# The timeline simulator for the scheduler, and the last layer's Hyena and GLA gates projected early and parked in DRAM

## The chip, the cores and the metric

The kernel runs on one core of one Trainium2 chip. The metric is the device time of one execution in microseconds. The kernel before took 2607.05 us in the median of three runs (2606.05 to 2609.52). One further execution was profiled.

## The reference, cut to what matters

Two layers work on 256 latent and 256 context tokens of width 1024. Each layer is a half-step SwiGLU, then four token mixers side by side on one normalised input `u` (MLA, GLA, GQA and Hyena, in the code the branches a, b, c and d with the indices 0 to 3), then an output projection and a second half-step SwiGLU. What matters here is how the four mixers are merged:

```python
def merge(outs, gate_cols, w_branch):
    B, L, _ = gate_cols.shape
    g = jax.nn.sigmoid(gate_cols.reshape(B, L, N_BRANCH, D_MODEL))
    y = g[:, :, 0] * (outs[0] @ w_branch[0])
    for i in range(1, N_BRANCH):
        y = y + g[:, :, i] * (outs[i] @ w_branch[i])
    return y
```

`gate_cols` is a product of `u` with 4096 columns of the input projection. So a gate depends on `u` alone and not on its branch, while `outs[i] @ w_branch[i]` has to wait for the branch. In the last layer only the 256 latent tokens are merged.

## The kernel before, in words

All activations lie with channels on the partitions (eight tiles of 128 channels for the width of 1024). Every fp32 product is made of three matmuls of rounded halves (`mm3`, line 296): weight high by input high, high by low, low by high. So each weight has to be split on the chip. `weights` (L323) loads a raw tile of 128x1024 with a DMA of the SP queue (`raw`, L318, three buffers `wr`) and `pieces` (L328) splits it in two pieces of 512 columns: ScalarE casts the high part `wh` (L311), and a subtraction makes the low part `wl` (L312). There are eight buffers for each of the two. The subtraction runs on VectorE, or on GpSimd for every piece while `self.share` is 1, as it is in the last layer beside the Hyena and GLA chains and nowhere else.

`mixer` (L1339) orders a layer's mixers. In the last layer, `prep` projects what MLA, GLA and GQA need and runs beside the MLA and GQA chains. Then `weave` (L1326) runs two chains, `hyena` and `gla`, against a filler, `merges`: in each round it takes one step of each chain, issued with a priority 200 instructions earlier than its place (`first`), and one step of the filler. Hyena has 15 such steps and GLA 13. The filler has 16 steps: `merge` (L1294) of MLA (b = 0) and of GQA (b = 2), eight output tiles each. One step of `merge` in this layer (n = 256) is a gate projection of 24 matmuls with the two split pieces of its own weight, twelve matmuls of the branch product into the other half of the same PSUM bank, a tanh on ScalarE (L1314), and two operations of VectorE (L1316, L1319) that form (1 + tanh) times the product and add it to `y`. After the weave come, with nothing beside them, `merge` of Hyena (b = 3) and of GLA (b = 1), 16 steps again, and then the output projection `wo`.

The gates' PSUM tiles come from a pool of two banks (`acc0`); the tanh's result lies in a pool `m` of three buffers. Weight loads, spills to DRAM and reloads from DRAM all go through the SP queue.

The order of the instructions on each engine is not written by hand: the tile framework's scheduler lays them out when the program is built. It takes the instructions by priority (their place in the program, moved by `first` and `evac`) as a simulator says that their operands and buffers are ready. Each engine then runs its list strictly in that order.

Of the kernel before, what the change touches and what calls it, by code (L numbers as in the profile page):

```python
# [8 lines left out]
F32 = mybir.dt.float32  # L9
# [3 lines left out]
AF = mybir.ActivationFunctionType  # L13
ALU = mybir.AluOpType
# [3 lines left out]
P = 128  # L18
D = 1024
KD = 8  # L20
L = 256
# [198 lines left out]
class Net:  # L220
# [150 lines left out]
    def load(self):  # L371
        nc, A, c = self.nc, self.A, self.const

        def ld(name, shape, src, dt=F32):
            t = c.tile(shape, dt, name=name)
            nc.sync.dma_start(out=t, in_=src)
            return t

        cc = ld("cc", [P, KD, 2], A["cc"])
        vec = ld("vec", [P, NVEC], A["vec"])  # L380
        self.v = {n: vec[:, o:o + w] for n, (o, w) in VEC.items()}
        self.ident = ld("ident", [P, P], A["ident"])
        tab = ld("tab", [P, NTAB], A["tab"])
        self.tab = {n: tab[:, o:o + w] for n, (o, w) in TAB.items()}
        self.ones = c.tile([P, 1], F32, name="ones")
        nc.vector.memset(self.ones, 1.0)
        cs = c.tile([P, KD, 32], F32, name="cs")
        nc.vector.memset(cs, 0.0)
        th = c.tile([P, KD, 2], F32, name="th")
        nc.scalar.activation(th, cc, AF.Tanh, scale=0.5)  # L390
        nc.vector.tensor_scalar(out=th, in0=th, scalar1=1.0, scalar2=0.5, op0=ALU.add, op1=ALU.mult)
        nc.vector.tensor_mul(cs[:, :, 0:2], th, cc)
        self.cs = cs
        self.xd = [self.dram.tile([KD, P, NT], F32, name=f"xd{l}") for l in range(DEPTH)]
        self.sp = {}
        self.hs = self.dram.tile([DEPTH, 2, 4, P, 512], F32, name="hs")

    def load_x(self, src, n=NT):
# [892 lines left out]
        out.extend(dst)  # L1291


    def merge(self, l, b, ob, u, n, first=False, last=None):  # L1294
        nc, A = self.nc, self.A
        if first:
            self.y = self.packed("y", "y", n, KD)
        for mp in range(4):
            wb = self.weights(A["w_br"][l, b, mp], 1024)
            for e in range(2):  # L1300
                m = 2 * mp + e
                pg = self.psa(0, "gate")
                self.fm(pg, self.weights(A["w_gate"][l, b * KD + m], 1024), u, n)
                t = self.tl("m", "mt")
                if n == NT:
                    nc.scalar.activation(t[:, :n], pg[:, :n], AF.Tanh, scale=0.5)
                    p = self.psa(1, "br")
                else:
                    p = pg[:, n:]
                for k in range(4):  # L1310
                    self.mm3(p[:, :n], wb(e * 512 + k * P, P), (ob[k][0][:, :n], ob[k][1][:, :n]), k == 0, k == 3)
                with self.evac():
                    if n < NT:
                        nc.scalar.activation(t[:, :n], pg[:, :n], AF.Tanh, scale=0.5)  # L1314
                    y = self.y[m]
                    nc.vector.scalar_tensor_tensor(out=y if first else t[:, :n], in0=t[:, :n], scalar=1.0, in1=p[:, :n],  # L1316
                                                   op0=ALU.add, op1=ALU.mult)
                    if not first:
                        nc.vector.tensor_add(y, y, t[:, :n])  # L1319
                if last is not None:  # L1320
                    h, lo = self.pair("yh", "yh", n, "yl")
                    self.two(h[:, :n], lo[:, :n], y)
                    last.append((h, lo))
                yield

    def weave(self, chains, fill):  # L1326

        chains = list(chains)
        more = True
        while chains or more:  # L1330
            for c in list(chains):
                with self.first():
                    self.ahead = AHEAD
                    if next(c, 0) is not None:
                        chains.remove(c)
                    self.ahead = 0
            more = next(fill, 0) is None

    def mixer(self, l, u, last):  # L1339
        nseq = 1 if last else 2  # L1340
        self.phase("end" if last else "mix")
        nq, n = 2 * nseq, nseq * L
        oa, ob, oc, od, y = [], [], [], [], []
        if last:
            self.phase("end", "end1")
            prep = self.prep(l, u, nq)
            for _ in range(2 * HEAD):
                next(prep)
            self.weave([self.mla(l, nq, oa), self.gqa(l, nq, oc)], prep)
            self.phase("end", "end2")  # L1350
            self.share = SHARE_W

            def merges():
                yield from self.merge(l, 0, oa, u, n, first=True)
                yield from self.merge(l, 2, oc, u, n)

            self.weave([self.hyena(l, u, nseq, od), self.gla(l, nq, ob)], merges())
            self.share = 0
            for _ in self.merge(l, 3, od, u, n):
                pass  # L1360
        else:
            self.weave([self.hyena(l, u, nseq, od)], self.prep(l, u, nq))
            self.weave([self.mla(l, nq, oa)], self.merge(l, 3, od, u, n, first=True))
            self.weave([self.gqa(l, nq, oc)], self.merge(l, 0, oa, u, n))
            self.weave([self.gla(l, nq, ob)], self.merge(l, 2, oc, u, n))
        for _ in self.merge(l, 1, ob, u, n, last=y):
            pass
        self.load_x(self.xd[l], n)
        gt = self.gate(l, 1, 0.5)
        for m in range(KD):  # L1370
            w = self.weights(self.A["w_out"][l, m], 1024)
            p = self.psa(m % 2, "wo")
            self.fm(p, w, lambda k, c0, c1: (y[k][0][:, c0:c1], y[k][1][:, c0:c1]), n)
            self.resid(p, m, n, gt)
# [58 lines left out]
```

## Time and profile before

| what | value |
|---|---|
| median of three runs | 2607.05 us (2606.05 to 2609.52) |
| profiled execution, its own time | 2601.85 us |
| its span, first to last instruction | 2600.1 us |
| TensorE matmul busy | 2497.5 us (96%) |
| VectorE busy | 1696.6 us (65%) |
| ScalarE busy | 1091.1 us (42%) |
| GpSimd busy | 264.9 us (10%) |
| mean granted TensorE clock | 0.986 |

The profile is of one execution. PE stands for TensorE's matmuls, PEld for its weight loads, which overlap them, DVE for VectorE, ACT for ScalarE, POOL for GpSimd, SP for SyncE, which issues the DMAs. Times in rows are microseconds from the start of the span unless marked ns; `x` counts instructions. "a<-b" names the tile written and the tiles read. The program's names are kept: `gate` is the PSUM tile of a merge step, `dp` a Hyena projection, `AT`, `obT`, `pre`, `la` and `ab` belong to GLA, `Z`, `yi` and `yT` to Hyena.

### The profile page before, as it was taken

The page shows a single profiled execution, that of the slowest core. Times are in us where ns is not written, and L with a number is a line of the kernel's source. Part 1 is how long each engine was busy: PE and PEld are TensorE (multiplying, and loading weights), DVE is VectorE, ACT ScalarE, POOL GpSimd, SP SyncE. Part 2 cuts the span into 40 slices and gives each one's busy share as a digit, 9 for nine tenths or more (in the row PEclk, how much of TensorE's full clock was granted, in tenths as well). Part 3 has the DMA queues.
Part 4 walks back from the last instruction along what each step waited for, and adds up shares of the span by engine and source line. Part 5 has one row for each costly group of instructions (what it writes and reads, how often), then busy time and mean ns, then how long its engine had stood idle before and what let it go on. Part 6 is the DMA issues. An engine that isn't in the chain of part 4 may idle for free. (4 is left out here: it accounts for less than half of the span.)

```text
span 2600.1 us, 36866 instructions
## 1 busy us (share of the span) xinstructions
PE 2497.5 (96%) x13624; PEld 2058.8 (79%) x13624; DVE 1696.6 (65%) x3377; ACT 1091.1 (42%) x2127; POOL 264.9 (10%) x240
## 2 busy tenths in 40 slices
PE   6999999999999999999999999999999987899998
PEld 4778887887877667777888878888888777788998
DVE  5667858577547778746744466767458667776665
ACT  4333223333545554433232343232346664455554
POOL 2110003001000000020000030000020147401000
PEclk9999999999999999999999999999999999899999
DMA  7564535332313123245623244545353333356554
GB/s 253 176 213 170 190 128 192 134 108 100 126 57 122 61 88 106 89 156 174 205 97 97 86 158 146 178 146 174 102 187 130 114 120 122 114 161 210 177 184 124
DMA packets 122371, 369.01 MB, mean 142 GB/s; under 512 B 14090, under 2 KB 19660, under 8 KB 122192
## 3 DMA queue, kind: packets, MB, share of 16 engines
q1 hardware_dynamic: 122192, 366.66, 42.8%
q8 instruction: 107, 1.75, 0.3%
q14 instruction: 72, 0.59, 0.1%
HBM read 346.16 MB, written 20.45 MB: 141 GB/s over the span
## 5 line engine op out<-in xcount | busy, mean ns | idle before, releaser
L311 ACT CAST wh<-wr 128x512 fp32r<-128x512 f32 (+1 forms) x926 | 564.0, 613 | 1070.3 <-PE gu L301 396.0
L312 DVE TENSOR_TENSOR wl<-wr,wh 128x512 fp32r<-128x512 f32 (+1 forms) x854 | 577.1, 682 | 410.1 <-ACT wh L311 399.3
L301 PE MATMUL gu<-ul,wh 128*128 128x512 f32 (+1 forms) x1408 | 514.7, 366 | 2.5 <-DVE ul L542 2.5
L301 PE MATMUL gu<-uh,wh 128*128 128x512 f32 (+1 forms) x1408 | 512.3, 366 | 2.4 <-ACT uh L536 2.3
L301 PE MATMUL gu<-uh,wl 128*128 128x512 f32 (+1 forms) x1408 | 511.5, 364 | 1.3 <-DVE wl L312 1.3
L301 PE MATMUL dn<-hh,wh 128*128 128x512 f32 (+1 forms) x1408 | 389.5, 363 | 0.0
L301 PEld LDWEIGHTS gu<-ul,wh 128*128 128x128 f32 x1408 | 265.7, 189 | 58.4 <-DVE ul L542 9.3
L301 PEld LDWEIGHTS gu<-uh,wh 128*128 128x128 f32 x1408 | 265.8, 189 | 52.0 <-ACT uh L536 7.2
L301 PEld LDWEIGHTS gu<-uh,wl 128*128 128x128 f32 x1408 | 265.6, 189 | 44.0 <-DVE wl L312 1.7
L301 PEld LDWEIGHTS dn<-hh,wh 128*128 128x128 f32 x1408 | 252.6, 188 | 41.3
L301 PE MATMUL dn<-hh,wl 128*128 128x512 f32 (+1 forms) x704 | 255.3, 363 | 0.0
L502 POOL TENSOR_TENSOR nacc<-nacc,sq 128x512 f32<-128x512 f32 (+1 forms) x39 | 46.2, 1185 | 1745.1 <-ACT sq L500 1736.7
L301 PE MATMUL gate<-uh,wh 128*128 128x256 f32 (+1 forms) x768 | 202.3, 328 | 3.3 <-DVE y L1316 3.3
L464 DVE SCALAR_TENSOR_TENSOR aj<-aw,crow 128x1024 bf16<-128x1024 f32 x160 | 193.7, 1224 | 0.0
L301 PE MATMUL gate<-uh,wl 128*128 128x512 f32 (+1 forms) x512 | 177.0, 346 | 4.3 <-POOL wl L312 2.8
L301 PEld LDWEIGHTS dn<-hh,wl 128*128 128x128 f32 x704 | 132.3, 188 | 20.4
L301 PEld LDWEIGHTS gate<-uh,wh 128*128 128x128 f32 x768 | 132.0, 195 | 15.4 <-DVE y L1316 3.5
L301 PE MATMUL tm<-wh,uh 128*128 128x256 f32 x576 | 140.3, 288 | 1.6 <-ACT uh L536 1.0
L312 POOL TENSOR_TENSOR wl<-wr,wh 128x512 fp32r<-128x512 f32 x72 | 106.4, 1489 | 239.9 <-ACT wh L311 234.1
L301 PE MATMUL tm<-wl,uh 128*128 128x256 f32 x432 | 124.1, 287 | 0.0
L301 PEld LDWEIGHTS gate<-uh,wl 128*128 128x128 f32 x512 | 99.1, 194 | 15.9 <-POOL wl L312 3.0
L642 DVE SCALAR_TENSOR_TENSOR x<-dn,gt,x 128x256 f32<-128x256 f32 x168 | 74.4, 478 | 54.6 <-PE dn L301 54.6
(408 smaller groups left out, 3975.7 us busy)
## 6 DMA issues: line engine op xcount, KB each, us to landing
wr<-in_gu SPq DMA_DIRECT2D x176, 512.0 KB, 3.5
aw<-in_adat SPq DMA_DIRECT2D x80, 512.0 KB, 3.6
wr<-in_dn SPq DMA_DIRECT2D x64, 512.0 KB, 3.6
wr<-in_w_gate SPq DMA_DIRECT2D x64, 512.0 KB, 3.5
aw<-in_ada SPq DMA_DIRECT2D x48, 512.0 KB, 4.6
wr<-in_w_tm SPq DMA_DIRECT2D x36, 512.0 KB, 3.6
wr<-in_w_br SPq DMA_DIRECT2D x32, 512.0 KB, 3.5
wr<-in_dn SPq DMA_DIRECT2D x32, 384.0 KB, 3.2
```

Of the source, the lines that this page charges most:

```text
L301: self.nc.tensor.matmul(out, l, r, start=start, stop=stop)
L311: self.nc.scalar.copy(h, src)
L312: (eng or self.nc.vector).tensor_sub(l, src, h)
L464: nc.vector.scalar_tensor_tensor(out=x, in0=w, scalar=1.0, in1=self.crow[s], op0=ALU.mult, op1=ALU.mult, accum_out=o[:, s:s + 1])
L502: (nc.vector if first and k % 2 else nc.gpsimd).tensor_add(acc[:, :n], acc[:, :n], sq[:, :n])
L642: self.nc.vector.scalar_tensor_tensor(out=self.x[m][:, c], in0=p[:, c], scalar=gt[:, m, s:s + 1], in1=self.x[m][:, c], op0=ALU.mult, op1=A ...
```

## The change

Three things change. The scheduler is told to use its timeline simulator (`schedule_with_timeline_sim=True`). In the last layer, a new generator `gates` projects the gates of Hyena (b = 3) and GLA (b = 1) as part of the filler: one gate step behind each merge step, so the filler has 32 steps, and `weave` takes two in each round. Each gate's tanh is stored to a DRAM tile `gd`. Behind the weave, `merge_gated` takes the place of `merge` for those two branches: it loads the tanh back and has only the branch's twelve matmuls for each output tile, in PSUM tiles of alternating pools. The first layer calls what it called before.

```diff
@@ Net.load
-        self.sp = {}
+        self.sp, self.gd = {}, {}
@@ Net
+    def gates(self, l, b, u, n):
+
+        self.gd[b] = self.dram.tile([KD, P, L], F32, name=f"gd{l}{b}")
+        for m in range(KD):
+            p = self.psa(0, "gate")
+            self.fm(p, self.weights(self.A["w_gate"][l, b * KD + m], 1024), u, n)
+            t = self.tl("m", "gt")
+            self.nc.scalar.activation(t[:, :n], p[:, :n], AF.Tanh, scale=0.5)
+            self.nc.sync.dma_start(out=self.gd[b][m], in_=t[:, :n])
+            yield
+
+    def merge_gated(self, l, b, ob, n, last=None):
+
+        nc = self.nc
+        for mp in range(4):
+            wb = self.weights(self.A["w_br"][l, b, mp], 1024)
+            for e in range(2):
+                m = 2 * mp + e
+                t = self.ld(self.tl("m", "mt")[:, :n], self.gd[b][m])
+                p = self.psa(e, "br")
+                for k in range(4):
+                    self.mm3(p[:, :n], wb(e * 512 + k * P, P), (ob[k][0][:, :n], ob[k][1][:, :n]), k == 0, k == 3)
+                y = self.y[m]
+                with self.evac():
+                    nc.vector.scalar_tensor_tensor(out=t, in0=t, scalar=1.0, in1=p[:, :n], op0=ALU.add, op1=ALU.mult)
+                    nc.vector.tensor_add(y, y, t)
+                if last is not None:
+                    h, lo = self.pair("yh", "yh", n, "yl")
+                    self.two(h[:, :n], lo[:, :n], y)
+                    last.append((h, lo))
+
@@ Net.weave
-    def weave(self, chains, fill):
+    def weave(self, chains, fill, width=1):
...
-            more = next(fill, 0) is None
+            for _ in range(width):
+                more = next(fill, 0) is None
@@ Net.mixer, the last layer
             def merges():
-                yield from self.merge(l, 0, oa, u, n, first=True)
-                yield from self.merge(l, 2, oc, u, n)
-
-            self.weave([self.hyena(l, u, nseq, od), self.gla(l, nq, ob)], merges())
+
+                for b, x, later in ((0, oa, 3), (2, oc, 1)):
+                    g = self.gates(l, later, u, n)
+                    for _ in self.merge(l, b, x, u, n, first=b == 0):
+                        yield
+                        next(g)
+                        yield
+
+            self.weave([self.hyena(l, u, nseq, od), self.gla(l, nq, ob)], merges(), 2)
             self.share = 0
-            for _ in self.merge(l, 3, od, u, n):
-                pass
+            self.merge_gated(l, 3, od, n)
+            self.merge_gated(l, 1, ob, n, last=y)
...
-        for _ in self.merge(l, 1, ob, u, n, last=y):
-            pass
+        if not last:
+            for _ in self.merge(l, 1, ob, u, n, last=y):
+                pass
@@ kernel
-    with tile.TileContext(nc, ) as tc:
+    with tile.TileContext(nc, schedule_with_timeline_sim=True) as tc:
```

## Rows read from the trace of the kernel before

**Rows 1.** Page, part 1: TensorE's busy time, share of the span, instructions

```profile
PE 2497.5 (96%) x13624; PEld 2058.8 (79%) x13624; DVE 1696.6 (65%) x3377; ACT 1091.1 (42%) x2127; POOL 264.9 (10%) x240
```

**Rows 2.** Stretches: length, PE, PEld, DVE, ACT, POOL busy, PE clock, DMA share, GB/s

```profile
450.00:1105.00 655.00, 640.14 (x3459) 505.25 (x3460) 451.73 (x967) 310.95 (x662) 19.12 (x21) 0.99 0.30 98
...
1160.00:1900.00 740.00, 738.91 (x3256) 599.14 (x3256) 434.07 (x789) 239.88 (x406) 37.96 (x42) 1.00 0.44 145
...
1950.00:2085.00 135.00, 129.16 (x863) 104.90 (x861) 98.11 (x252) 87.66 (x225) 9.26 (x7) 0.99 0.37 121
2085.00:2292.00 207.00, 169.59 (x1179) 149.84 (x1177) 154.64 (x294) 102.68 (x202) 103.89 (x69) 0.92 0.35 113
2292.00:2360.00 68.00, 67.63 (x563) 67.63 (x564) 48.51 (x90) 36.83 (x72) 0.00 (x0) 1.00 0.62 197
```

**Rows 3.** TensorE's waits from 2085 to 2292: us in total, times, longest

```profile
PE AT L301 <- DVE ab L1015: 7.1, 2, 4.3
PE obT L348 <- DVE z L1071: 6.3, 3, 3.3
PE AT L301 <- issue: 4.3, 1, 4.3
PE gate L301 <- DVE y L1316: 3.3, 1, 3.3
...
PE gate L301 <- POOL wl L312: 2.8, 1, 2.8
```

**Rows 4.** The `gate` tile alone, two stretches: length, then PE, PEld, DVE, ACT busy

```profile
2085.00:2292.00 207.00, 85.95 (x592) 79.72 (x592) 6.62 (x16) 6.06 (x16) 0.92 0.35 113
2292.00:2360.00 68.00, 67.45 (x560) 67.24 (x560) 6.18 (x15) 5.66 (x15) 1.00 0.62 197
```

**Rows 5.** GpSimd's splits, 2085 to 2292: count | busy, mean ns | idle before, its releasers

```profile
L312 POOL TENSOR_TENSOR wl<-wr,wh 128x512 fp32r<-128x512 f32 x65 | 97.1, 1507 | 87.2 <-ACT wh L311 81.4 <-PE dp L301 2.1 <-issue 1.8
```

**Rows 6.** The tile `wl`, GpSimd's instructions: ns min/median/max, first and last start

```profile
L312 POOL TENSOR_TENSOR wl<-wr,wh x72: 1257/1292/5724, 2053.1 to 2268.5; 128x512 fp32r<-128x512 f32 x72
```

**Rows 7.** Three of VectorE's groups in GLA, last layer, 2085 to 2292

```profile
L1008 DVE TENSOR_TENSOR la<-ab 64x512 f32<-64x512 f32 x8 | 12.4, 1555 | 0.2
L1000 DVE TENSOR_TENSOR_SCAN ab<-scan,la 64x512 f32<-64x512 f32 x4 | 8.5, 2132 | 0.1
...
L998 DVE TENSOR_TENSOR_SCAN ab<-scan,la 64x512 f32<-64x512 f32 x4 | 6.8, 1704 | 0.1
```

**Rows 8.** The same three groups in the first layer's GLA, 900 to 1060

```profile
L1008 DVE TENSOR_TENSOR la<-ab 64x512 f32<-64x512 f32 x8 | 5.5, 686 | 0.2
L1000 DVE TENSOR_TENSOR_SCAN ab<-scan,la 64x512 f32<-64x512 f32 x4 | 4.9, 1222 | 0.1
L998 DVE TENSOR_TENSOR_SCAN ab<-scan,la 64x512 f32<-64x512 f32 x4 | 4.8, 1212 | 0.1
```

**Rows 9.** The chain that ended last, one piece: start us, us, what

```profile
2292.37 67.45 PE gate L301 x560
```

**Rows 10.** VectorE's merge groups, 2292 to 2384

```profile
L1319 DVE TENSOR_TENSOR y<-y,mt 128x256 f32<-128x256 f32 x16 | 6.8, 425 | 0.5
L1316 DVE SCALAR_TENSOR_TENSOR mt<-mt,gate 128x256 f32<-128x256 f32 x16 | 6.6, 412 | 0.7 <-ACT mt L1314 0.7
```

**Rows 11.** DMA issues: count, KB each, median us from issue to landing

```profile
kd<-sp_bk SPq DMA_DIRECT2D x16, 128.0 KB, 4.5
...
x<-xd SPq DMA_DIRECT2D x8, 128.0 KB, 3.3
```

**Rows 12.** The SP queue's largest wait, 2085 to 2292: us in total, times, longest

```profile
SPq L320 <- POOL wl L312: 143.7, 31, 20.8
```

**Rows 13.** ScalarE's table loads at one line, 2085 to 2292

```profile
L994 ACT ACT_TABLE_LOAD x4 | 5.1, 1283 | 0.1
```

## The prediction, made before the changed kernel was run

> **What bounds the kernel now.** The page's first part comes first: TensorE's matmuls are busy for 2497.5 us of a span of 2600.1 us [rows 1], so about 103 us are all that better order could give back. The table of stretches shows where they lie [rows 2]. The feed-forward stretch from 1160 to 1900 idles for 1.1 us of 740. The first layer's mixers (450 to 1105) idle for 14.9 of 655, and the last layer's MLA and GQA beside `prep` (1950 to 2085) for 5.8 of 135. The stretch this change is about, Hyena and GLA beside the merges (2085 to 2292), idles for 37.4 of 207, and its granted clock is 0.92 of 2.4 GHz. The 68 us behind it, the merges of Hyena and GLA, leave TensorE no gap: they are pure matmul time.
>
> The list of TensorE's waits tells what the 37.4 us are [rows 3]. They are waits for operations of the chains (GLA's `AT` and `obT` above all), few and long, up to 4.3 us each. GpSimd's splits aren't what TensorE lacks: GpSimd itself is idle for 87.2 us there, waiting for ScalarE's casts [rows 5]. So weights for the filler mostly lie ready, but stand behind a chain's instruction in TensorE's fixed order.
>
> The second thing to see is a slower price per matmul. The `gate` tile's 592 matmuls took 85.95 us inside the weave, 0.1452 us each; behind it 560 took 67.45, 0.1204 us each [rows 4]. The difference times 592 is 14.6 us, most of it the lower clock.
>
> **The tail gets shorter: minus 37.5 us.** The chain's piece of 560 `gate` matmuls, 67.45 us [rows 9], holds 16 steps of twelve branch matmuls, 192 in all. The other 368 are gate projections: 368 x 0.1204 = 44.3 us that move into the weave (the sixteen missing from 384 already ran there). The 192 that stay need 23.1 us. But each step now reads its gate back from DRAM into one of three buffers, and a buffer comes free when VectorE has used it. A round trip is the landing of 128 KB, 3.3 to 4.5 us [rows 11], and the two merge operations, 0.41 + 0.43 us [rows 10]: 4.1 to 5.3 us, by three buffers 1.4 to 1.8 us a step against 1.44 of matmuls. That makes 23 to 28.5 us for 16 steps; I take the upper end, since the branch weights' loads share the queue, and 1.5 us more because the last step's additions and split before `wo` have less matmul time to hide behind. 67.5 - 30 = 37.5 us saved. The bounds are 39 (28.5 us) and 43 (24.6 us) in one direction and some 32 in the other, if the loads land 1 us later.
>
> **The weave gets longer: plus 13.3 us.** TensorE's work there at the tail's price is 169.6 - 14.6 = 155.0 us, and with the moved gates 199.3 us. To that come three terms.
>
> - Waits. The gates put 44.3 / 16 = 2.8 us of further matmuls in each filler step. A wait of up to 2.8 us can vanish behind them; of those shown four exceed it, by 4 us in all [rows 3]. I carry 6 us.
> - GpSimd. The 16 moved weights bring 32 splits, which in the tail were VectorE's and here are GpSimd's. GpSimd's splits and VectorE's operations hold each other up: three GLA operations that took 686, 1222 and 1212 ns in the first layer, where GpSimd splits nothing, took 1555, 2132 and 1704 ns here [rows 7, 8]. That is 8 x 0.87 + 4 x 0.91 + 4 x 0.49 = 12.6 us on VectorE, and on GpSimd 65 x (1.507 - 1.292) = 14.0 us over the median [rows 5, 6]. Together 26.6 us by 65 splits is 0.41 us a split, and 32 x 0.41 = 13.1 us. I put all of it on the path, since the waits in rows 3 end with VectorE.
> - The clock. It still falls at the waits that stay: 2 us of the 14.6.
>
> 199.3 + 6 + 13.1 + 2 = 220.4 us against 207. The bounds: 207.3 without any blocking, and 255.5 if each split delays the chains by its whole mean of 1.507 us.
>
> Here a page speaks against the change. The Trainium skill, "SBUF — State Buffer", section "Who interferes with whom", says that a VectorE instruction with two SBUF inputs and a GpSimd instruction that reads SBUF exclude each other for a whole instruction, so that one of them "fully blocks". By that rule at its worst a split of 1292 ns would cost the chains 1292 ns, 41.3 us for 32, and the sum would come out at +4.1 us instead of -24.2. The rows above bear the blocking out (a maximum of 5724 ns for one split [rows 6]), but at a third of that price on average.
>
> **What I cost at nothing.** The 16 stores of a tanh wait on SP for ScalarE, and the weight loads behind them wait too; the splits would feel it. But SP's loads already stand for 143.7 us waiting for a free `wr` buffer behind GpSimd [rows 12], so three raw weights and eight pieces lie ahead of TensorE. If that cover is gone, one store costs up to the 2.8 us that its gate takes. The 16 tanhs only change place, unless one falls while GLA's logarithm holds ScalarE's table: then two loads of 1.28 us, at most four times, 10 us [rows 13], on an engine half idle there [rows 2]. ScalarE's 32 casts move with the splits, at the same price.
>
> **The simulator.** The parameter relays every engine's list, and no row of before shows what that does. It can't gain much elsewhere: 14.9 + 5.8 us in the two other woven stretches. It can lose: if the first layer's mixers idled at the 4.3% of 1950 to 2085 instead of 2.3%, 13 us; at the 18% of 2085 to 2292, 103 us. Where the program is one row of matmuls, as from 1160 to 1900, the order hardly matters. I take 0, by the nearest rows, for those stretches idle little under the present order, and keep +13 and -10 in the range.
>
> **Sum.** -37.5 + 13.3 = -24.2 us, so 2577.7 for the profiled execution of 2601.85. The median of the runs stood 5.2 us above that execution, so 2583.
>
> **The rivals.**
>
> - *GpSimd's splits hold the chains up* (slower). Place: GLA's gate operations between `pre` and `AT`. Price: 1.507 us a split, 255.5 us of weave, +11 in sum, 2618 us. It decides from 1.16 us a split, where 32 splits eat the 37.2 us that are left. For it: VectorE was busy for 155 of 207 us [rows 2], so a split nearly always meets something. Against it: the 0.41 us measured.
> - *The gaps stay.* The order still puts a chain's instruction ahead of ready filler, and the gates run in addition: 169.6 + 44.3 + 37.4 = 251.3 us, +6.8 in sum, 2614 us; with 7 us of waits covered there is no change. For it: today the filler was ready and didn't fill the gaps. Against it: more matmuls now stand between two instructions of a chain, whichever order is chosen.
> - *The order gets worse in the first layer's mixers*: 2583 + 13 = 2596 us, and more if it is worse than that.
> - *All of it is absorbed*: a weave of 207.3 us and a tail at the matmuls' price, -42.6 us, 2564 us. For it: the clock's 14.6 us come back with denser work. Against it: rows 7.
> - The parameter does nothing: the same sum as the forecast, since I took 0.
>
> **How the numbers follow.** A measurement here tells about 0.2%, 5 us. The forecast has 0.50, all absorbed 0.13, a worse first layer 0.15, gaps that stay 0.12, GpSimd 0.10. The range takes in all but the ends: 2560 (absorbed, with a few us from the simulator) to 2614. Faster than 2602: the forecast, all absorbed, and under a third of the third case, 0.67. Within 5 us: partly covered gaps, 0.09. Slower: the rest, 0.24.
>
> **What would show it.** In the changed profile the 560-matmul piece should be 192 matmuls in 25 to 30 us, with TensorE waiting for `mt`, or VectorE, in between; GpSimd should have some 32 splits more; the weave should end 10 to 20 us later, with TensorE's share there up from 82% to over 90% and its clock near 1.00; the `AT` and `obT` waits should shrink to about 6 us. I am wrong if the weave grows by 35 us or more, if GLA's operations at L1008 grow past 2 us, or if TensorE's idle time from 450 to 1105 moves by over 10 us.

## The result, and the profile after

The changed kernel takes 2644.81 us in the median of four runs (2644.72 to 2648.64), the kernel before 2608.28 us on the same chip. The ratio is 1.0141, with a 95% interval of 1.0124 to 1.0159. So it is 1.4% slower, where 2583 us and at the most 2614 us were forecast. The profiled run took 2648.64 us, its span 2646.7 us.

Part 1 and three rows of part 2 of the page of the changed kernel, to be read beside [rows 1]:

```profile
PE 2495.8 (94%) x13624; PEld 2078.6 (79%) x13624; DVE 1680.8 (64%) x3345; ACT 1089.2 (41%) x2127; POOL 300.6 (11%) x272
...
PE   7999999999999997699999999999999889788998
...
PEclk9999999999999999699999999999999989899999
```

The same two rows of the kernel before:

```profile
PE   6999999999999999999999999999999987899998
...
PEclk9999999999999999999999999999999999899999
```

TensorE does the same 13624 matmuls in the same busy time; GpSimd has the 32 further splits that were expected. The 46.6 us by which the span grew are idle time of TensorE. The row of slices shows where: the digits 7 and 6 around 1050 us (a slice is 66 us), and the eights and the seven from 2050 us on. The first lies in the first layer, whose program text the change doesn't touch.

The starts of `wo` (the output projection) and the end of `dn` (the last matmuls of the feed-forward) part the span into four stages. The first two columns are the pair under study, the other two the first two experiments below, in us:

| stage | before | after | gates alone | simulator alone |
|---|---|---|---|---|
| start to the first layer's `wo` | 1108.3 | 1147.0 | 1108.8 | 1148.6 |
| from there to the end of `dn` | 792.0 | 797.8 | 792.1 | 797.8 |
| from there to the last layer's `wo` | 459.4 | 459.4 | 466.5 | 482.9 |
| from there to the end | 240.4 | 242.5 | 243.5 | 242.1 |

So 44.5 of the 46.6 us lie ahead of the last layer's mixers. In the two kernels with early gates the last layer's `wo` starts while VectorE still forms the last tiles of `y`, and stands still between its first matmuls (in the changed kernel it runs without a gap from 2405.9 us, not from 2404.2). So what the gates bring is read from the last two rows together.

TensorE's waits of the changed kernel, the longest (us in total, times, longest):

```profile
PE AT L301 <- issue: 29.3, 3, 10.6
PE ada L301 <- DMA aw<-in_ada: 19.3, 6, 12.5
PE Og L301 <- DVE STl L1053: 12.3, 3, 4.2
```

The first and the third belong to GLA; the longest piece of the second stands at the very start, where the kernel before waits 14.0 us for something else. In the first layer's mixers alone the longest wait for `AT`, before and after:

```profile
PE AT L301 <- DVE ab L1015: 3.3, 3, 1.3
```

```profile
PE AT L301 <- issue: 21.3, 2, 10.6
```

The chain that ended last shows two of the waits for `AT` in the first layer (start, us, what):

```profile
1046.42 4.01 PE Og L301 x22
1050.43 10.61 issue
1061.04 2.08 PE AT L301 x16
...
1073.11 4.78 PE Og L301 x22
1077.88 10.61 issue
```

Between `Og` of one head and `AT` of the next stand GLA's gate operations on ScalarE and VectorE, and no filler stands there in TensorE's list. Some was left: 72 `gate` matmuls, which read `u` and their weights alone, run behind 1110 us, when GLA is done. In the kernel before this latency was there too, but filler matmuls stood in it. How much work each kernel had done when GLA began is in the table of stretches, first before, then after (length, then PE, PEld, DVE, ACT, POOL busy, PE clock, DMA share, GB/s):

```profile
445.60:950.00 504.40, 495.46 (x2697) 392.45 (x2698) 332.62 (x714) 244.35 (x552) 23.52 (x26) 0.99 0.30 98
950.00:1108.00 158.00, 152.03 (x793) 117.84 (x793) 123.41 (x259) 70.57 (x118) 0.00 (x0) 1.00 0.32 100
```

```profile
443.50:950.00 506.50, 491.91 (x2712) 406.56 (x2712) 325.90 (x688) 236.26 (x526) 23.43 (x26) 0.99 0.30 98
950.00:1147.00 197.00, 154.88 (x779) 117.18 (x778) 131.41 (x284) 78.49 (x146) 0.00 (x0) 0.86 0.25 77
1050.00:1100.00 50.00, 20.32 (x127) 14.46 (x124) 35.07 (x86) 16.87 (x26) 0.00 (x0) 0.64 0.09 27
```

By 950 us both had done the same amount, 2697 and 2712 matmuls. But GLA's first matmul, `pre`, came at 950.7 us before and at 981.1 us after (tile `pre`, again before and after: ns min, median, max, first and last start):

```profile
L301 PE MATMUL pre<-lr,wlg x4: 476/488/504, 950.7 to 1027.6; 128*128 128x512 f32 x4
```

```profile
L301 PE MATMUL pre<-lr,wlg x4: 389/477/503, 981.1 to 1066.0; 128*128 128x512 f32 x4
```

So in the simulator's order TensorE had done more filler by 950 us (504 `gate` matmuls against 415) and less of the chains. GLA's chain was 30 us late, and what filler remained didn't cover it: 779 matmuls took 197 us, where 793 had taken 158. The instruction lists of the two programs say the same without any clock: ahead of GLA's four groups of `AT` stand 45, 98, 93 and 82 filler matmuls before, and 73, 124, 18 and 6 after (for the last three groups the traces agree within five).

Hyena and GLA in the last layer, the stretch the change is about (to be read beside [rows 2]):

```profile
1990.00:2170.00 180.00, 162.04 (x1086) 132.98 (x1085) 116.63 (x285) 113.78 (x278) 24.05 (x19) 0.95 0.35 115
2170.00:2378.00 208.00, 182.40 (x1351) 172.38 (x1350) 142.31 (x263) 102.91 (x199) 123.27 (x90) 0.90 0.46 152
2378.00:2406.00 28.00, 25.54 (x203) 24.66 (x203) 22.04 (x52) 12.73 (x25) 0.00 (x0) 1.00 0.60 195
```

The tail did shrink, to 28 us with `wo`'s first matmuls in it. But the weave still idles for 26 us at a clock of 0.90, and the stretch of MLA and GQA ahead of it now idles for 18 us of 180, against 5.8 of 135.

### The profile page after: what moved, and what is told of

It reads as the page before. It is cut to its first block, busy times and chain, and to the rows that moved or that the text cites. A ratio compares the mean times of both kernels' runs of the same rounds, so it can differ in the third digit from the quotient of the medians.

```text
span 2646.7 us, 37033 instructions
## 1 busy us (share of the span) xinstructions
PE 2495.8 (94%) x13624; PEld 2078.6 (79%) x13624; DVE 1680.8 (64%) x3345; ACT 1089.2 (41%) x2127; POOL 300.6 (11%) x272
## 4 chain that ended last, share of the span: by engine, by line
PE 88%; DVE 5%; ACT 3%; issue 2%; DMA 2%; POOL 0%; SPq 0%; DVEq 0%; ACTq 0%; POOLq 0%
PE gu L301 32%; PE dn L301 16%; PE gate L301 10%; PE tm L301 6%; PE dp L301 4%; PE br L301 4%; PE wo L301 2%; PE ada L301 2%; PE O L301 2%; PE S L301 2%; PE PT L348 1%; DMA aw<-in_ada 1%; PE bk L301 1%; PE Og L301 1%; PE Z L301 1%
## 5 line engine op out<-in xcount | busy, mean ns | idle before, releaser
L312 DVE TENSOR_TENSOR wl<-wr,wh 128x512 fp32r<-128x512 f32 (+1 forms) x822 | 565.0, 692 | 436.0 <-ACT wh L311 417.1
L312 POOL TENSOR_TENSOR wl<-wr,wh 128x512 fp32r<-128x512 f32 x104 | 140.1, 1362 | 247.4 <-ACT wh L311 235.4
```

Source lines behind the costliest of these rows:

```text
L312: (eng or self.nc.vector).tensor_sub(l, src, h)
```

## The experiments

Each run is compared with the kernel before on the same chip. Theory A was that the loss is the simulator's order; theory B that it comes with the gates.

**The gates alone**, with the scheduler as before:

```diff
-    with tile.TileContext(nc, schedule_with_timeline_sim=True) as tc:
+    with tile.TileContext(nc, ) as tc:
```

> The early gates with the scheduler's simulator left as it was before. Theory A, the simulator's new order is what costs: the first layer runs as before (TensorE idle about 15 us from 450 to 1105, its output projection from about 1108 us on), and the gates bring some 24 us, so about 2583 us; 2565 to 2600 fits. Theory B, the early gates cost by themselves, through GpSimd's 32 further splits: 2615 us or more, with the whole loss behind 2085 us.

2612.68 us, ratio 1.0029 [1.0018, 1.0040]. The first layer is as before (`wo` at 1108.8 us). But the gates bring nothing here either, and neither theory's range was met. The table of stretches, and the piece of the chain behind Hyena and GLA:

```profile
2086.00:2321.00 235.00, 194.41 (x1348) 177.25 (x1344) 160.74 (x277) 114.59 (x224) 132.27 (x92) 0.91 0.39 128
2321.00:2344.00 23.00, 23.00 (x194) 23.00 (x193) 10.68 (x21) 12.49 (x26) 11.73 (x9) 1.00 0.58 195
2344.00:2371.00 27.00, 26.22 (x214) 25.64 (x213) 22.69 (x55) 13.50 (x26) 0.00 (x0) 1.00 0.72 235
```

```profile
2321.17 23.04 PE gate L301 x192
```

The stretch beside the chains ends 29 us later than before, TensorE idles beside them for 40.6 us (37.4 before), and 192 of the 384 gate matmuls stand behind the chains, alone.

**The simulator alone**, on the kernel before:

```diff
-    with tile.TileContext(nc, ) as tc:
+    with tile.TileContext(nc, schedule_with_timeline_sim=True) as tc:
```

> The kernel before with nothing but the scheduler's timeline simulator switched on. Theory A: the first layer's output projection starts near 1147 us as in the changed kernel, 39 us late, and GLA's last heads run with TensorE idle; the last layer's weave is reordered too, so 2640 to 2670 us in all. Theory B: within 10 us of 2608.

2670.0 us, ratio 1.0242 [1.0227, 1.0258]. The parameter by itself costs more than the whole change: theory A. By the stage table it loses 40.3 us in the first layer, 5.8 in the feed-forward and 23.5 in the last layer's mixers. (In the feed-forward of the changed kernel TensorE waits 3.2 us for `aw`, a DMA, where it did not before, and 2.0 us for `uh`, 0.4 before.) Under its order the gates then bring 23.1 us (the last two rows of the table, 725.0 to 701.9); under the old one they cost 10.2 (699.8 to 710.0).

**The chains' weights first** (theory C: GpSimd takes Hyena's splits too late, behind the gates'), on the gates alone:

```diff
-                    self.ahead = AHEAD
+                    self.ahead = 0 if width > 1 else AHEAD
```

> The early gates under the old simulator, and the splits of Hyena's own weights (dp) and of its tables issued with the chain's priority in the last weave instead of the filler's. Theory C, in the early-gates kernel the dp splits stand behind the gates' splits, dp comes late, and VectorE, in order, stands 23.5 us before the convolution at L1193: that wait falls below 10 us, the weave shortens by 15 to 25 us, 2585 to 2600 us in all. Theory L, GpSimd and VectorE block each other: no change, 2608 to 2618.

2609.79 us, ratio 1.0019 [1.0009, 1.0030]: C falls. The wait that it named, VectorE's at L1193, went from 23.5 to 11.8 us, but 167 gate matmuls still stand behind the chains. The run showed something else: its tail is held by the read-back, as the chain that ended last says:

```profile
2350.05 3.39 DMA mt<-gd
2353.47 0.43 DVE mt L1318
2353.92 0.44 DVE y L1319
2354.38 4.98 DMA mt<-gd
```

**The gates' splits on VectorE**, on the gates alone:

```diff
-            self.fm(p, self.weights(self.A["w_gate"][l, b * KD + m], 1024), u, n)
+            share, self.share = self.share, 0
+            w = self.weights(self.A["w_gate"][l, b * KD + m], 1024)
+            self.share = share
+            self.fm(p, w, u, n)
```

> The early gates under the old simulator, with the gates' 32 splits on VectorE instead of GpSimd. Theory L: the mutual blocking of the further splits goes, GLA's operation at L1008 stays at or below 1156 ns, and the weave shortens by 10 to 15 us, so 2596 to 2603. Theory C: what counts is the order of the casts and splits; GpSimd has only the dp and merge splits, which helps a little, while VectorE takes 22 us more in a chain that hangs on VectorE: 2608 to 2620.

2596.88 us, ratio 0.9968 [0.9954, 0.9981]. These 32 splits cost 16 us on GpSimd, 0.49 us each, over what they cost on VectorE. The chains end at 2299 us instead of 2321.

**Four filler steps in each round** (theory P: the gates stand too late in the program), on the gates alone, `weave(..., 4)` for `weave(..., 2)`:

> The early gates under the old simulator, four filler steps a round instead of two. Theory P, the filler is paced by its place in the program, and that alone leaves the 192 gate matmuls (23 us) behind the chains: they vanish, and the total falls by 10 to 23 us, 2590 to 2603. Theory C: the gates' splits crowd the chain's even more; the matmuls left behind shrink but the weave grows by as much or more, 2610 to 2630.

2631.21 us, ratio 1.0101 [1.0083, 1.0119]: P falls. No gate is left behind, but the weave takes 278 us; the chains wait for the filler: VectorE stands 34.5 us before operations of the filler (`y` and `mt` at L1347) that lack their tanh.

**A larger lead for the chains under the simulator** (theory R: the lead is too small for its order), on the changed kernel:

```diff
-AHEAD = 200
+AHEAD = 800
```

> The changed kernel with the chains' priority 800 instead of 200 instructions ahead. Theory R, under the timeline simulator the filler overtakes the chains because their lead is too small, and GLA's last heads run alone: the first layer's output projection comes back to 1110 to 1130 us and the total to 2605 to 2630. Theory S, a chain's instruction is placed late because the simulator holds it ready late, whatever its priority: the output projection stays within 8 us of 1147, the total within 10 us of 2645.

2648.27 us, ratio 1.0167 [1.0150, 1.0185], the first layer's `wo` again at 1147.0 us. R falls. The filler ahead of GLA's four `AT` groups stays as it was (in the trace 124, 17 and 6 ahead of the last three, the same as in the changed kernel's).

**Three things together** under the old order: the gates' splits on VectorE, the chains' weights first, and the read-back into two pools in turn:

```diff
-                t = self.ld(self.tl("m", "mt")[:, :n], self.gd[b][m])
+                t = self.ld(self.tl(("m", "za")[e], "mt")[:, :n], self.gd[b][m])
...
-                    self.ahead = AHEAD
+                    self.ahead = 0 if width > 1 else AHEAD
```

> The version that the runs so far point to: old simulator, early gates split on VectorE, Hyena's own splits at the chain's priority, and the parked gates read back into seven buffers instead of three. Against the kernel before: 0.32% for VectorE's splits as measured, some 2 us for the priority, 3 to 5 us for the read-back, so 0.5% faster, about 2592 where the kernel before takes 2605. If the read-back isn't what holds the tail, the tail stays at 27 us and the sum at 2595 to 2599.

2598.49 us, ratio 0.9965 [0.9955, 0.9976], no better than the gates' splits alone. The tail's 192 `br` matmuls now run without a gap:

```profile
2333.22 23.04 PE br L301 x192
```

With three buffers they took from 23.4 us (the gates alone) to 26.1 us (the changed kernel), so the read-back cost at most some 3 us there. But the chains ended at 2310 us instead of 2299, and the tail began at 2333 instead of 2321.

**The gates' splits on VectorE under the simulator**, the same edit on the changed kernel:

> The changed kernel with the gates' 32 splits on VectorE. Theory Q, GpSimd is the slower queue, at 1.44 us a split against 0.69, and the chain's splits stand in it behind the gates': 10 to 16 us faster than the changed kernel here too, 2629 to 2635. Theory S2, the timeline simulator already lays the chains out later than their splits are ready: no gain, 2640 to 2650.

2644.44 us, ratio 1.0155 [1.0133, 1.0176]. What gave 16 us under the old order gives nothing here.

**No split on GpSimd at all**, on the gates alone:

```diff
-SHARE_W = 1
+SHARE_W = 0
```

> The early gates under the old simulator with no split on GpSimd at all. Theory L, mutual blocking of GpSimd and VectorE is the price: GLA's operation at L1008 falls from 1156 to about 690 ns, VectorE's and GpSimd's waits for each other go, 2580 to 2592. Theory Q: the waits for dp's splits fall below 1 us, but VectorE takes 65 further splits of 0.69 us, 45 us on top of 158 in a weave of 213, and becomes the bound: 2600 to 2620.

2578.68 us, ratio 0.9902 [0.9883, 0.9921]: faster than both kernels. GLA's operations of [rows 7] now take as long as in the first layer [rows 8]; the gates alone, the gates' splits on VectorE, and this run (`L1008` of GLA: busy, mean ns):

```profile
L1008 DVE TENSOR_TENSOR la<-ab 64x512 f32<-64x512 f32 x8 | 9.2, 1156 | 0.2
```

```profile
L1008 DVE TENSOR_TENSOR la<-ab 64x512 f32<-64x512 f32 x8 | 9.3, 1158 | 0.2
```

```profile
L1008 DVE TENSOR_TENSOR la<-ab 64x512 f32<-64x512 f32 x8 | 5.5, 685 | 0.2
L1000 DVE TENSOR_TENSOR_SCAN ab<-scan,la 64x512 f32<-64x512 f32 x4 | 4.9, 1220 | 0.1
L998 DVE TENSOR_TENSOR_SCAN ab<-scan,la 64x512 f32<-64x512 f32 x4 | 4.8, 1212 | 0.1
```

A group's mean doesn't follow the number of splits: 1156 and 1158 ns with and without the gates' 32. The time does: the ratios are 1.0029, 0.9968 and 0.9902 with 104, 72 and no splits on GpSimd in the last layer. With none left, TensorE waits at most 2.9 us for any one thing in the weave.

**Only Hyena's gates early**, on the run with the gates' splits on VectorE; GLA's are merged behind the weave as before:

```diff
-                for b, x, later in ((0, oa, 3), (2, oc, 1)):
-                    g = self.gates(l, later, u, n)
+                g = self.gates(l, 3, u, n)
+                for b, x in ((0, oa), (2, oc)):
...
-                        next(g)
+                        if i % 2:
+                            next(g)
...
```

> The early gates under the old simulator, split on VectorE, but Hyena's eight only; GLA's are projected in its merge as before. Of all sixteen, 189 of 384 gate matmuls were left behind the chains. Theory V, the weave takes only about eight gates whatever is offered, and the rest costs its own matmul time in either place: the same as with sixteen, 2592 to 2600. Theory W, each gate offered slows the chains: 2582 to 2590, with the weave below 205 us. Theory X, all sixteen are needed: 2602 or more.

2604.7 us, ratio 1.0002 [0.9987, 1.0017]. With Hyena's eight gates alone the gain is gone, as in theory X; GLA's eight alone were not tried.

**No split on GpSimd, without the gates**: the kernel before with `SHARE_W = 0`.

> The kernel before (old order, no gates parked), with no split on GpSimd. It parts the gain of the version with the gates and no GpSimd split (ratio 0.9902) in two. Theory L, each GpSimd split has a price of its own for the chains: the gates' version lost 34 us by 104 splits, 0.33 us each, so the 72 of the kernel before cost it 24 us, and taking them away gives about 2581, ratio 0.989 to 0.993; the parked gates would then bring only the last few us. Theory T, both are needed: without the gates the stretch beside Hyena and GLA has only 155 us of matmuls at the tail's price against chains that last 190 us or more, so a faster chain leaves TensorE idle all the same and the tail stays 68 us: 2592 to 2604, ratio 0.995 to 0.9995, the stretch from Hyena's first projection to the tail 10 us shorter at most.

2594.02 us, ratio 0.9949 [0.9935, 0.9962], inside theory T's 2592 to 2604 us and well above L's 2581. So of the 0.98% of the version with both, the splits' engine brings 0.51 and the gates on top of it 0.47. With the splits on GpSimd the same gates cost 0.29.

**Filler held back beside GLA, under the simulator.** Three small VectorE operations add zero times a chain's output to the gates' input, so that the filler behind them can't be placed earlier. The values stay as they are.

```diff
+            def hold(o):
+                x = u(0, 0, n)[1]
+                self.nc.vector.scalar_tensor_tensor(out=x, in0=o[1][:, :n], scalar=0.0, in1=x, op0=ALU.mult, op1=ALU.add)
...
-            self.weave([self.gla(l, nq, ob)], self.merge(l, 2, oc, u, n))
+            self.weave([self.gla(l, nq, ob)], held())
```

> The changed kernel, its first layer's filler beside GLA held back by three small VectorE operations that add zero times a chain's output (GQA's last, GLA's first and second) to the input of the gate projections, so that no order can place these matmuls earlier. In the program's lists the filler matmuls ahead of GLA's four AT groups are then 62, 76, 63, 95, against 73, 124, 18, 6 in the changed kernel and 45, 98, 93, 82 in the kernel before. Theory F, the first layer loses because its filler runs out ahead of GLA's last heads: the first layer's mixers come back from 697 us to 655 to 670, TensorE's issue wait ahead of AT from 29 us to under 8, and the whole is 2608 to 2620, ratio 1.001 to 1.006. Theory O, the simulator's order costs MLA and GQA as much, and GLA's idle time is only where it shows: the mixers stay above 685 us, the whole above 2632, ratio 1.011 or more.

2641.06 us, ratio 1.0131 [1.0117, 1.0145]. `wo` came at 1138.6 instead of 1147.0 us: theory F, that only GLA's last heads lack filler, falls, and theory O's numbers are met. TensorE's idle time behind 950 us halved (21.3 us, 42.1 in the changed kernel), but ahead of it there are now 25.0 us for 14.6.

**Filler held back beside all three chains**, nine such operations (the expectation says ten) spread over MLA, GQA and GLA:

```diff
+            self.weave([self.mla(l, nq, oa)], held(self.merge(l, 3, od, u, n, first=True), oa, {2: 1, 4: 2, 6: 3}))
+            self.weave([self.gqa(l, nq, oc)], held(self.merge(l, 0, oa, u, n), oc, {5: 1, 6: 2, 7: 3}))
+            self.weave([self.gla(l, nq, ob)], held(self.merge(l, 2, oc, u, n), ob, {5: 1, 7: 2}, oc[-1]))
```

> The changed kernel, with the first layer's filler held back along all three of its chains (MLA, GQA and GLA) by ten small VectorE operations of the kind of the run before. In the program's lists the filler matmuls inside MLA's eight groups of scores go from 33, 39, 123, 38, 40, 12, 6, 0 (the changed kernel) to 0, 0, 47, 25, 47, 25, 48, 44 (before: 15, 7, 87, 6, 65, 10, 25, 10), those ahead of GQA's first score from 258 to 160 (before 194). Theory O, the simulator's order lets the filler run ahead in each chain, stretches the chain and has none left behind it; held in GLA alone the idle time only moved: the first layer's mixers come to 655 to 672 us from 703.5, MLA's scores from 125 to 100 to 112 us, the whole to 2605 to 2618, ratio 1.000 to 1.005. Theory E, the loss is the order of the other engines' lists (VectorE's and ScalarE's), which no pace of the filler mends: the mixers stay above 688 us, the whole above 2632, ratio 1.010 or more.

2640.16 us, ratio 1.0132 [1.0112, 1.0151]: what theory E gave as its sign, and theory O's numbers are missed. The stretches and GLA's first tile:

```profile
443.50:950.00 506.50, 478.98 (x2638) 392.49 (x2637) 330.97 (x709) 236.86 (x537) 23.63 (x27) 0.98 0.28 94
950.00:1143.00 193.00, 171.33 (x849) 133.26 (x849) 131.70 (x274) 78.14 (x135) 0.00 (x0) 0.92 0.27 89
```

```profile
L301 PE MATMUL pre<-lr,wlg x4: 389/486/793, 967.5 to 1050.8; 128*128 128x512 f32 x4
```

GLA starts 13.6 us earlier than in the changed kernel. But now 74 matmuls fewer are done by 950 us, and the idle time has moved ahead of GLA (27.5 us until 950, 14.6 in the changed kernel). This doesn't prove E: the fences themselves hold filler back where it could have run, and they don't set which instruction stands ahead of which within a step.

**The same without a split on GpSimd**, `SHARE_W = 0`:

> The same with no split on GpSimd in the last layer. If the two losses are separate, this gains over the run beside it what the split's engine gained under the old order with gates (34 us, from 2612.7 to 2578.7): 2572 to 2584 where the other comes to 2605 to 2618, ratio 0.987 to 0.992. If the last layer's 24 us of the simulator's order lie in its own early filler and not in the splits, the gain is under 12 us: as the gates' 32 splits moved to VectorE gained nothing under the simulator's order (ratio 1.0155).

2633.97 us, ratio 1.0125 [1.0091, 1.0158], 6 us below the run beside it and not 34. The loss in the last layer isn't tied to the splits either: without any, the simulator's order still takes 449.1 us from the end of `dn` to the last `wo`, the old one 433.3 in the run with gates and no split.

## Why the prediction was wrong, by its steps

**The step that failed is "The simulator … I take 0, by the nearest rows, for those stretches idle little under the present order."** Alone the parameter costs 63.7 us (2670.0 against 2606.27). With that in place of 0 the sum would have been +39.5 us, near the +36.5 measured, so this term makes the miss. The little idle time of a stretch, 14.9 us of 655, bounds what a better order can gain there; of what a worse one can lose it says nothing. The text had the other end in hand, 103 us at the idle share of Hyena and GLA, but kept only 13 of it for the range. The rival that came true, a worse order in the first layer's mixers, was given 0.15 and 13 us. It measured 40.3 us in the first layer in the run of the simulator alone, and 23.5 us more in the last layer's mixers, which no rival had. The sign that was named, idle time from 450 to 1105 moving by over 10 us, is what shows: by the rows above it went from 14.9 us (8.9 up to 950 us and 6.0 behind) to 56.7 (14.6 and 42.1). The two other signs of being wrong did not come: beside the chains the changed kernel took 208 us, and L1008 took 999 ns in the mean there.

**What the order does** is shown: chains later and filler earlier, for the same number of matmuls by 950 us. Why the simulator puts them so isn't settled. It isn't the chains' lead (800 for 200 changes nothing), nor filler that lacks in GLA alone, nor the splits' engine. Holding the filler back won at most 5 us, but the fences idle TensorE themselves, so they don't clear the filler's pace. Whether VectorE's and ScalarE's lists or the fine order in TensorE's is to blame was not separated.

**The tail: forecast 30 us for the read-back and its 192 matmuls.** In the changed kernel the matmuls took 26.1 us (2378.1 to 2404.2), and `wo` ran without a gap 27.8 us after the first of them. The limit by three buffers is there, as its chain shows:

```profile
2385.82 3.41 DMA mt<-gd
...
2389.28 5.36 DMA mt<-gd
...
2395.23 4.55 PE br L301 x36
```

The landings on this chain and on that of the run with the chains' weights first took 2.74 to 5.36 us, around the 3.3 to 4.5 us of [rows 11]. But the limit doesn't always bind: with the gates alone the same 192 matmuls took 23.4 us (2344.0 to 2367.4) with the same three buffers, near the 23.1 us worked out for the matmuls.

**The gates in the sum: forecast -24.2 us, measured -23.1 under the simulator's order, +10.2 under the old one** (profiled executions; by the medians the second is +6.4, 2612.68 against 2606.27). (The weave's terms add up to +13.4 us and not +13.3, which changes nothing.) That the first agrees is in part luck, since the order it was summed on, that of rows 2 to 8, is the old one. There two assumptions fail. "A wait of up to 2.8 us can vanish behind them": the idle time in the weave went from 37.4 to 40.6 us with the gates alone. In the changed kernel TensorE's share there rose to 88% at a clock of 0.90, where over 90% and near 1.00 had been named. And "44.3 us that move into the weave": the order left 192 gate matmuls behind the chains. The rival that the gaps stay, with its 0.12, describes this better than the forecast does.

**GpSimd's price.** 0.41 us a split, 13.1 us for 32, was near for these splits: 16 us were measured, and 0.33 us a split from all 104 (34 us). The rival's 1.507 us didn't come. But a split has no fixed price, and part of this agreement is luck: the kernel before, from whose rows the 0.41 was worked out as 26.6 us by 65 splits, gained only 12.5 us when its 72 splits moved (2606.55 to 2594.02), 0.17 us each. Nor do the means of the blocked operations give the price, since those means stayed alike in two runs that lay 16 us apart.

By the Trainium skill, "SBUF — State Buffer", section "Who interferes with whom", a VectorE instruction with two inputs in SBUF and a GpSimd instruction that reads SBUF exclude each other. The rows agree in kind: with no split on GpSimd `L1008` falls from 1156 to 685 ns. The worst case that the prediction worked out by this rule, an estimate of 41.3 us for 32 splits, was not reached.

## What to carry to other kernels

A parameter that relays every engine's list is a change of the whole program: price it by what the idle share of its worst stretch would cost elsewhere, and run it alone, since here it hid what the gates did. A stretch that idles little may owe that to its order, and then has much to lose. And before more work is put beside a chain, look at what feeds that work: the same gates cost 0.29% with their splits on GpSimd and brought 0.47% without.

## What the runs showed of the hardware

With GLA alone TensorE was busy for 20.3 of 50 us, its granted clock was 0.64 of 2.4 GHz, so for most of the time it stood at the lower of its two levels, 1.2 GHz, and the first layer's transposes `obT` took 418 ns in the median where they had taken 272 (before, then after):

```profile
L348 PE MATMUL obT<-ident,z x16: 270/272/330, 985.5 to 1072.0; 128*128 128x128 f32 x16
```

```profile
L348 PE MATMUL obT<-ident,z x16: 270/418/473, 1035.3 to 1108.8; 128*128 128x128 f32 x16
```

So idle time costs twice: from 950 us to `wo` the clock averaged 0.86 against 1.00 before.

In the kernel before without GpSimd's splits TensorE ran the same matmuls beside the last layer's chains (1178 from 2085 to 2286 us, 1179 from 2085 to 2292 with the splits). It idled less, 25.8 us instead of 37.4, and yet its granted clock was lower, 0.86 instead of 0.92, so that the matmuls were busy for 175.2 us instead of 169.6. The idle time of a whole stretch doesn't tell the clock in it.
